# Two-stage normalising tiles, a last FFN-out block by interleaved token halves, and a ring of their own for the queries, in a one-core transformer layer

## The chip, the cores and the metric

The kernel runs on one core of a Trainium2 chip. The metric is the device time of one execution in microseconds (us). A profiled execution gives the trace; several others give the times.

## The reference, cut to what matters

One layer with D = 1024, 512 latent tokens and 256 context tokens, batch 1, in float32. What the change touches is queries and keys, the gates of the recurrence, the second norm with its SwiGLU feed-forward network (FFN) of width 2816, and the final norm:

```python
qk = silu(short_conv(concat([q, k]), conv_w, conv_b))     # 4 heads of 256
S  = einsum('bhtd,bhsd->bhts', q, k) * exp(Dm - m)        # scores of a chunk
x  = x + g1 * (mix @ w_out)
h  = rmsnorm(x, norm_ffn) * (1 + sc2) + sh2
g, u = split(h @ w_ffn_in, 2)
x  = x + g2 * ((silu(g) * u) @ w_ffn_out)                 # width 2816 = 22 tiles of 128
out = rmsnorm(x, norm_final)
```

## The kernel before, in words

**Products.** Activations lie transposed: 128 features on the partitions, 512 tokens in the row. Every factor is split into a high part, rounded by ScalarE's copy to the matmul's format, and a low part, the rest, subtracted on VectorE. A product is then three matmuls, high by high, high by low, low by high (`mm3`, L181 to L183). Matmuls move 512 columns (all tokens) or 256 (one half of them, `HALF[0]` or `HALF[1]`).

**Weights.** `wload` (line 145) has SyncE load a tile into the ring `wr` of three, ScalarE round it (L151, L164, L170) and VectorE subtract (L152, L165, L171). Its target is the ring `wh`/`wl` of two, the ring `gh`/`gl` of two ("wide"), or half tiles of `oh`/`ol`, five of each. Tiles of all these rings start at multiples of 256 bytes. Some are read from 48 elements (192 bytes) further on: the value weights (`vload`, `skip`) and the big tile `hp` of the normalised FFN input. A ring's slot is given again when all readers of its tile are done.

**Order.** Most instructions are put in order by a planner, engine by engine, from the program order and its own idea of when each is ready. Inside `manual_schedule` (the first stage, lines 242 to 364, and the first part of the FFN, lines 1091 to 1152) TensorE, ScalarE and VectorE run in the order in which the program is written; DMAs remain the planner's. On the chip each engine takes its instructions in that fixed order.

**Attention.** For each of four heads: `values`, `keys`, `attention` (two score stages, `scores`, L699 to L701, 36 matmuls of 256 columns each, key tile loaded, query tile moved), then the pooled branch, and `queries` and `keys` of the next head. Queries and keys share the ring `kq` of eleven 512-column tiles; a head takes four for its queries and six for its keys. `late_mod` streams the rows of `w_ada`, 512 KB at a time, into `pb` and multiplies them on VectorE (L496). `gates` works on small tiles [128 x 48], each with a place of its own, and writes `g_rows` to DRAM, from where `decays` reads it back.

**FFN-in.** `norm_tile(k, c, r, full)` makes one 128 x 256 tile of the normalised input: VectorE multiplies (L910), ScalarE adds the shift and rounds (L912, the high part), VectorE subtracts (L913, the low part), ScalarE writes the unrounded tile (L914). It runs eight times for the first half of the tokens under the planner, and eight times for the second half inside the manual stretch (lines 1102 to 1105). The first three of 22 feed-forward tiles run there, each by halves (`Half`: gate, up, silu, mul, low). Then come the others, by one level of Strassen's scheme (`prepare`, `front`, `back`, `strassen`), seven products of 256 columns in place of eight. It needs sums of quarters of the input (`total`: N1, N2, T3, T4), each one VectorE pass and then one split on ScalarE and VectorE. The unrounded quarters "11" and "21" lie in the ring `ur` of two, in which `prepare` also loads one of its two weight tiles.

**FFN-out** follows in three blocks, after tiles 8, 15 and 22. `ffn_out(j, c, w, c0, c1)` multiplies one output tile, adds it into `x1` (L1166) and, in the last block, adds its square to the final norm's sum (`st2`, L206, L210). Six output tiles of the last block are run over all 512 columns, tiles 6 and 7 by halves. `final(i, sd)` normalises one half of the tokens (eight VectorE instructions, L1198) and stores it. The first half's `final` comes in the middle of the last product:

```python
    for j in (6, 7):
        ffn_out(j, HALF[0], wl_[j], c0, c1)
    ffn_out(6, HALF[1], wl_[6], c0, c1)
    sd = st2.rstd_cols(HALF[0])
    ffn_out(7, HALF[1], wl_[7], c0, c1, lambda: final(0, sd))
    final(1, st2.rstd_cols(HALF[1]))
```

Of the kernel before, what the change touches and what calls it, by code (L numbers as in the profile page):

```python
# [9 lines left out]
F32 = mybir.dt.float32  # L10
F32R = mybir.dt.float32r
# [19 lines left out]
BUFS = {"a": 24, "tmp": 7, "kq": 11, "E": 6, "Sp": 10, "m": 7, "pm": 4, "act": 16, "x1": 8, "oh": 5, "ol": 5}  # L31
# [17 lines left out]
def layer_kernel(ctx: ExitStack, tc, xT, cT, w0, w1, wv0, wv, wada_a, wada_b, par, crow, bg, wpool,  # L49
# [34 lines left out]
    open_pool("kqp", ("kq",))  # L84
# [57 lines left out]
    def wide(tag, bufs=2):  # L142
        return tl(tag, [P, D], F32R, bufs, LINE)

    def wload(src, n, dst=None, skip=0):

        raw = tl("wr", [P, WMAX], F32, 3)
        nc.sync.dma_start(raw[:, :n], src)
        if dst is None:
            wh, wl = (tl(t, [P, WMAX], F32R, 2, LINE)[:, skip:skip + n] for t in ("wh", "wl"))  # L150
            nc.scalar.copy(wh, raw[:, :n])  # L151
            V.tensor_sub(wl, raw[:, :n], wh.bitcast(F32))  # L152
            return [(wh[:, i * P:(i + 1) * P], wl[:, i * P:(i + 1) * P]) for i in range(n // P)], wh, wl
        if dst == "wide":
            h, l = wide("gh"), wide("gl")
            split(raw[:, :n], h[:, :n], l[:, :n])
            return [(h[:, i * P:(i + 1) * P], l[:, i * P:(i + 1) * P]) for i in range(n // P)], None, None
        if isinstance(dst, str):
            dst = (dst, dst)
        parts = []  # L160
        for c in range(0, n, T):
            m = min(T, n - c)
            h, l = (S(t, F32R) for t in dst)
            nc.scalar.copy(h[:, :m], raw[:, c:c + m])  # L164
            V.tensor_sub(l[:, :m], raw[:, c:c + m], h[:, :m].bitcast(F32))  # L165
            parts += [(h[:, i * P:(i + 1) * P], l[:, i * P:(i + 1) * P]) for i in range(m // P)]
        return parts, None, None
# [226 lines left out]
    def queries(h):  # L394
        return [conv_part(lat_tile(Q0 + 2 * h + dk), T, 2 * h + dk) for dk in range(2)]
# [158 lines left out]
    def gates():  # L554
# [7 lines left out]
        ab, u, w, w2, pl, lf = (E(n, (P, NGC)) for n in ("g_ab", "g_u", "g_w", "g_w2", "g_pl", "g_lf"))  # L562
# [44 lines left out]
        MLb = E("g_MLb")  # L607
# [14 lines left out]
        rows = E("g_rows", (32, P))  # L622
# [3 lines left out]
        gx, c1, em = E("g_gx"), E("g_c1"), E("g_em")  # L626
# [5 lines left out]
        G = E("g_G")  # L632
# [274 lines left out]
    def norm_tile(k, c, r, full):  # L907

        t = S("tmp")[:, :TC]
        V.scalar_tensor_tensor(t, x1[k][:, c], sc2[:, k:k + 1], r, ALU.mult, ALU.mult)  # L910
        h, l = hpart(c)[k]
        nc.scalar.activation(h, t, AF.Identity, bias=sh2[:, k:k + 1])  # L912
        V.scalar_tensor_tensor(l, t, sh2[:, k:k + 1], h.bitcast(F32), ALU.add, ALU.subtract)  # L913
        nc.scalar.activation(full, t, AF.Identity, bias=sh2[:, k:k + 1])  # L914
# [134 lines left out]
    whole = {"11": [tl("ur", [P, D], F32, 2)]}  # L1049
    whole["21"] = [tl("ur", [P, D], F32, 2)]  # L1050
    for nm in ("11", "21"):
        whole[nm] = [whole[nm][0][:, :T], whole[nm][0][:, T:]]
    r = st1.rstd_rows(sd, HALF[0])
    for k in range(KT):
        norm_tile(k, HALF[0], r, whole_at(("11", "21")[k // 4], k % 4))
# [35 lines left out]
    with tc.manual_schedule(engines={mybir.EngineType.PE, mybir.EngineType.Activation, mybir.EngineType.DVE}):  # L1091
# [10 lines left out]
        norm_tile(0, HALF[1], r, whole_at("12", 0))  # L1102
        e.low()
        for k in range(1, KT):
            norm_tile(k, HALF[1], r, whole_at(("12", "22")[k // 4], k % 4))
            if k == 4:
                f.silu()
# [8 lines left out]
        e.silu()  # L1116
        t3 = total(("12", T3), lambda i: V.tensor_sub(w12[i], w22[i], w12[i]))
        n2 = total(("22", N2), lambda i: V.scalar_tensor_tensor(w22[i], w11[i], -1.0, w22[i], ALU.mult, ALU.subtract))
        wg2 = wload(wffi[4], D)[0]
        e.mul()  # L1120
# [7 lines left out]
        t4 = total(("21", T4), lambda i: V.scalar_tensor_tensor(w21[i], w22[i], -1.0, w21[i], ALU.mult, ALU.subtract))  # L1128
# [7 lines left out]
        t3()  # L1136
# [3 lines left out]
        t4()  # L1140
# [16 lines left out]
    def ffn_out(j, c, w, c0, c1, after_first=None):  # L1157

        turn_[0] += 1
        acc = banks[turn_[0] % 3]  # L1160
        m = 4 if after_first else c1 - c0
        mm3(acc[:, c], w[:m], half(act[c0:c0 + m], c), last=m == c1 - c0)
        if after_first:
            after_first()
            mm3(acc[:, c], w[m:], half(act[c0 + m:c1], c), first=False)
# [5 lines left out]
    def wchunk(j, c0, c1, dst=None):  # L1171
        return wload(wffo[j][:, c0 * P:c1 * P], (c1 - c0) * P, dst)[0]
# [123 lines left out]
```

## Time and profile before

| | |
|---|---|
| median of 3 runs | 912.81 us (907.91 to 913.37) |
| profiled execution | 911.29 us, span of its instructions 909.5 us |
| TensorE (PE) busy | 881.7 us, 97% of the span |
| VectorE (DVE) busy | 613.0 us, 67% |
| ScalarE (ACT) busy | 428.1 us, 47% |
| DMA | 121.18 MB, 133 GB/s on average |
| mean granted TensorE clock | 0.992 of full |

Times in rows count from the span's first instruction. PE is TensorE's matmuls, PEld its weight loads, DVE VectorE, ACT ScalarE, POOL GpSimd, SP SyncE, which issues most DMAs. A bracket at a row's end is the engine's idle time just before it and what ended that. The shown end of a matmul is modelled and overlaps the next one; the spacing of starts is what counts.

### The profile page before, as it was taken

What the parts mean: (1) busy time and instruction counts of PE and PEld (TensorE: products, weight loads), DVE (VectorE), ACT (ScalarE), POOL (GpSimd) and SP (SyncE); (2) the same over time, 40 slices, a digit from 0 to 9 for tenths busy, and PEclk for the clock granted to TensorE, in tenths of its full rate; (3) what the DMA queues carried; (4) which work ended last, traced back from release to release, by engine and by line L of the source; (5) the groups of instructions that cost most, each with busy time, mean ns of one, the idle gap of its engine ahead of it and who ended that gap; (6) DMA issues with size and microseconds to landing.
All of it is one profiled execution on the core that took longest, in us unless ns stands there. A gap on an engine that the chain in (4) does not pass through costs nothing.

```text
span 909.5 us, 14723 instructions
## 1 busy us (share of the span) xinstructions
PE 881.7 (97%) x5757; PEld 793.9 (87%) x5757; DVE 613.0 (67%) x1188; ACT 428.1 (47%) x806; POOL 63.3 (7%) x92
## 2 busy tenths in 40 slices
PE   8999989999999999999999899999999999999995
PEld 7689888899888998889987798989789998899985
DVE  3678665856688666886778676785366754866454
ACT  4464353545343553335543356574145741666330
POOL 0000010010001000000000000020011100111000
PEclk9999999999999999999999999999999999999998
DMA  8843031322166312762048730485355643766222
GB/s 333 324 139 115 27 79 58 116 59 81 50 214 217 99 39 78 230 226 87 27 152 280 251 117 24 134 206 126 93 153 145 153 118 88 201 140 141 55 61 93
DMA packets 42485, 121.18 MB, mean 133 GB/s; under 512 B 4625, under 2 KB 9393, under 8 KB 41393
## 3 DMA queue, kind: packets, MB, share of 16 engines
q1 hardware_dynamic: 36944, 110.29, 37.4%
q0 software_dynamic: 5472, 9.96, 6.7%
q8 instruction: 45, 0.74, 0.3%
q14 instruction: 24, 0.19, 0.1%
HBM read 116.55 MB, written 3.69 MB: 132 GB/s over the span
## 4 chain that ended last, share of the span: by engine, by line
PE 73%; DVE 11%; DMA 9%; issue 3%; ACT 3%; POOL 0%; SPq 0%; POOLq 0%; DVEq 0%; ACTq 0%
PE ps L181 15%; PE ps L183 15%; PE ps L182 15%; DMA pb<-in_wada_b 7%; PE pat L326 3%; PE ps L538 2%; PE ps L539 2%; PE ps L537 2%; DVE wl L152 2%; PE pat L741 2%; PE pat L181 2%; PE pat L182 2%; PE pat L183 2%; PE pat L739 2%; PE pat L740 2%
## 5 line engine op out<-in xcount | busy, mean ns | idle before, releaser
L151 ACT CAST wh<-wr 128x1024 fp32r<-128x1024 f32 (+3 forms) x82 | 82.7, 1009 | 134.8 <-PE ps L182 94.8
L181 PE MATMUL ps<-a,wh 128*128 128x512 f32 (+1 forms) x368 | 138.8, 377 | 0.0
L182 PE MATMUL ps<-a,wh 128*128 128x512 f32 (+1 forms) x368 | 138.5, 376 | 0.0
L183 PE MATMUL ps<-a,wl 128*128 128x512 f32 (+1 forms) x368 | 138.4, 376 | 0.0
L152 DVE TENSOR_TENSOR wl<-wr,wh 128x1024 fp32r<-128x1024 f32 (+3 forms) x82 | 96.4, 1177 | 39.9 <-ACT wh L151 38.2
L183 PE MATMUL ps<-act,wl 128*128 128x512 f32 (+1 forms) x210 | 80.7, 384 | 3.3 <-DVE wl L152 3.3
L181 PE MATMUL ps<-act,wh 128*128 128x512 f32 (+1 forms) x210 | 80.5, 383 | 0.7 <-ACT wh L151 0.7
L182 PE MATMUL ps<-act,wh 128*128 128x512 f32 (+1 forms) x210 | 80.4, 383 | 0.0
L183 PEld LDWEIGHTS ps<-a,wl 128*128 128x128 f32 x368 | 69.3, 188 | 12.7
L181 PEld LDWEIGHTS ps<-a,wh 128*128 128x128 f32 x368 | 69.3, 188 | 12.0
L182 PEld LDWEIGHTS ps<-a,wh 128*128 128x128 f32 x368 | 69.3, 188 | 11.9
L538 PE MATMUL ps<-wl,a 128*128 128x256 f32 (+1 forms) x192 | 54.3, 283 | 2.6 <-DVE wl L152 2.5
L537 PE MATMUL ps<-wh,a 128*128 128x256 f32 (+1 forms) x192 | 54.1, 282 | 0.9 <-DVE tmp L374 0.9
L539 PE MATMUL ps<-wh,a 128*128 128x256 f32 (+1 forms) x192 | 54.0, 281 | 0.0
L957 POOL DMA_DIRECT2D ol<-in_wffi x38 | 33.5, 889 | 260.6 <-ACT ol L956 118.9
L181 PE MATMUL ps<-hp,gh 128*128 128x256 f32 x176 | 50.2, 285 | 0.9 <-ACT tmp L999 0.9
L183 PEld LDWEIGHTS ps<-act,wl 128*128 128x128 f32 x210 | 39.9, 190 | 11.9 <-DVE wl L152 4.6
L1166 DVE SCALAR_TENSOR_TENSOR x<-ps,lb,x 128x512 f32<-128x512 f32 (+1 forms) x26 | 18.4, 709 | 46.3 <-PE ps L183 46.3
L183 PE MATMUL ps<-hp,gl 128*128 128x256 f32 x176 | 49.1, 279 | 0.5 <-DVE gl L171 0.5
L182 PE MATMUL ps<-hp,gh 128*128 128x256 f32 x176 | 49.0, 279 | 0.0
L496 DVE SCALAR_TENSOR_TENSOR pb<-pb,crow_s 128x1024 f32<-128x1024 f32 x32 | 39.1, 1223 | 14.6 <-DMA pb<-in_wada_b 14.2
L181 PEld LDWEIGHTS ps<-act,wh 128*128 128x128 f32 x210 | 39.9, 190 | 8.5 <-ACT wh L151 1.2
(296 smaller groups left out, 2484.4 us busy)
## 6 DMA issues: line engine op xcount, KB each, us to landing
wr<-in_w SPq DMA_DIRECT2D x42, 512.0 KB, 3.5
pb<-in_wada_b SPq DMA_DIRECT2D x32, 512.0 KB, 4.5
wr<-in_wffi SPq DMA_DIRECT2D x25, 512.0 KB, 4.0
ur<-in_wffi SPq DMA_DIRECT2D x19, 512.0 KB, 4.0
ol<-in_wffi POOLq DMA_DIRECT2D x38, 256.0 KB, 5.1
ada<-in_wada_a SPq DMA_DIRECT2D x8, 1024.0 KB, 8.3
wr<-in_wffo SPq DMA_DIRECT2D x16, 448.0 KB, 3.4
x<-in_xT SPq DMA_DIRECT2D x16, 256.0 KB, 5.7
```

The source lines that it names most:

```text
L151: nc.scalar.copy(wh, raw[:, :n])
L152: V.tensor_sub(wl, raw[:, :n], wh.bitcast(F32))
L181: nc.tensor.matmul(dst, wh, ah, start=first and i == 0, stop=False, skip_group_check=on)
L182: nc.tensor.matmul(dst, wh, al, start=False, stop=False, skip_group_check=on)
L183: nc.tensor.matmul(dst, wl, ah, start=False, stop=last and i == n - 1, skip_group_check=on)
L326: nc.tensor.matmul(acc0[i], w_first[k][i][w], aT[k][x], start=k + w + x == 0, stop=k == KT - 1 and w == 1)
L496: V.scalar_tensor_tensor(wa[:, :D], wa[:, :D], 0.5, crow_s, ALU.mult, ALU.mult, accum_out=mods[:, i:i + 1])
L537: nc.tensor.matmul(acc[:, :n], ah, wh, start=kk == 0, stop=False)
L538: nc.tensor.matmul(acc[:, :n], ah, wl, start=False, stop=False)
L539: nc.tensor.matmul(acc[:, :n], al, wh, start=False, stop=kk == KT - 1)
L957: nc.gpsimd.dma_start(l, dram, accum_op=ALU.add)
L1166: V.scalar_tensor_tensor(x1[j][:, c], acc[:, c], g2[:, j:j + 1], x1[j][:, c], ALU.mult, ALU.add)
```

## The change

It has four parts.

1. The norm is cut into `norm_first` (L910's multiply) and `norm_rest`; in VectorE's order the multiply of tile k+1 now stands ahead of the low part of tile k, and ScalarE writes the unrounded tile ahead of that low part.
2. The unrounded quarters "11" and "21" move from `ur` to the tile `sg`. T4's sum is written to two tiles of `tmp`, ahead of `e.mul`, and the splits of T3 and T4 come ahead of the second `f.mul`, no longer inside the first `prepare`. `e.silu` comes after two of the sums.
3. Queries get a ring `q` of four tiles, read from 48 elements on; `kq` shrinks from eleven to seven. To make room, `gates` uses five of its small tiles a second time, and `g_rows` becomes a tile of `tmp`.
4. In the last FFN-out block all eight weight tiles are loaded into places in which they stay for both halves; all products run by halves of 256 columns, interleaved, and the first half's `final` stands ahead of two whole products. Six of the eight weight tiles start 16 elements (64 bytes) into their places; tiles 4 and 5, in `oh`/`ol`, don't.

```diff
-BUFS = {... "kq": 11, ...}
+BUFS = {... "kq": 7, "q": 4, ...}
@@ wload
-            h, l = wide("gh"), wide("gl")
-            split(raw[:, :n], h[:, :n], l[:, :n])
+            h, l = (wide(t)[:, skip:skip + n] for t in ("gh", "gl"))
+            split(raw[:, :n], h, l)
@@ queries
-        return [conv_part(lat_tile(Q0 + 2 * h + dk), T, 2 * h + dk) for dk in range(2)]
+        return [conv_part(lat_tile(Q0 + 2 * h + dk), T, 2 * h + dk,
+                          [tl("q", [P, T + NEXT], F32R, BUFS["q"], LINE)[:, NEXT:] for _ in range(2)]) for dk in range(2)]
@@ gates
+        free = [E(n) for n in ("g_ab", "g_u", "g_w", "g_w2", "g_pl")]
+        ab, u, w, w2, pl = (flat(t) for t in free)
-        MLb = E("g_MLb")
+        MLb = free[0]
-        rows = E("g_rows", (32, P))
+        rows = S("tmp")[:32, :P]
-        gx, c1, em = E("g_gx"), E("g_c1"), E("g_em")
+        gx, c1, em = free[1:4]
-        G = E("g_G")
+        G = free[4]
@@ FFN-in
+    def norm_first(k, c, r):
         t = S("tmp")[:, :TC]
         V.scalar_tensor_tensor(t, x1[k][:, c], sc2[:, k:k + 1], r, ALU.mult, ALU.mult)
+        return t
+    def norm_rest(k, c, t, full, between):
         h, l = hpart(c)[k]
         nc.scalar.activation(h, t, AF.Identity, bias=sh2[:, k:k + 1])
+        nc.scalar.activation(full, t, AF.Identity, bias=sh2[:, k:k + 1])
+        t2 = between()
         V.scalar_tensor_tensor(l, t, sh2[:, k:k + 1], h.bitcast(F32), ALU.add, ALU.subtract)
-        nc.scalar.activation(full, t, AF.Identity, bias=sh2[:, k:k + 1])
+        return t2
+    def norm_tiles(c, r, at, also=lambda k: None):
+        t = norm_first(0, c, r)
+        for k in range(KT):
+            t = norm_rest(k, c, t, at(k), lambda: norm_first(k + 1, c, r) if k < KT - 1 else None)
+            also(k)
...
-    whole = {"11": [tl("ur", [P, D], F32, 2)]}
-    whole["21"] = [tl("ur", [P, D], F32, 2)]
+    sg0 = tl("sg", [P, 2 * D], F32, 1, LINE)
+    whole = {nm: [sg0[:, (2 * q + i) * T:(2 * q + i + 1) * T] for i in range(2)] for q, nm in enumerate(("11", "21"))}
...
         n1()
-        e.silu()
         t3 = total(("12", T3), ...)
         n2 = total(("22", N2), ...)
+        e.silu()
         wg2 = wload(wffi[4], D)[0]
+        whole["t4"] = [S("tmp") for _ in range(2)]
+        t4 = total(("t4", T4), lambda i: V.scalar_tensor_tensor(whole["t4"][i], w22[i], -1.0, w21[i], ALU.mult, ALU.subtract))
         e.mul()
...
         pw.append((wg2, wload(wffi[5], D)[0], act_tiles(2)))
-        t4 = total(("21", T4), ...)
+        t3()
+        t4()
         f.mul()
...
         p = prepare(NP)
         next(p)
-        t3()
         next(p)
         e.silu()
         next(p)
-        t4()
         e.mul()
@@ last FFN-out block
-    for j in range(6):
-        ffn_out(j, ALL, wchunk(j, c0, c1), c0, c1)
-    wl_ = {j: wchunk(j, c0, c1, ("oh", "ol")) for j in (6, 7)}
+    wl_ = [wchunk(j, c0, c1, (None, None, "wide", "wide", ("oh", "ol"), ("oh", "ol"), None, None)[j], 16) for j in range(KT)]
+    for j in range(4):
+        ffn_out(j, HALF[0], wl_[j], c0, c1)
+    for j in range(4):
+        ffn_out(j, HALF[1], wl_[j], c0, c1)
+        ffn_out(j + 4, HALF[0], wl_[j + 4], c0, c1)
+    ffn_out(4, HALF[1], wl_[4], c0, c1)
+    sd = st2.rstd_cols(HALF[0])
+    ffn_out(5, HALF[1], wl_[5], c0, c1)
+    final(0, sd)
     for j in (6, 7):
-        ffn_out(j, HALF[0], wl_[j], c0, c1)
-    ffn_out(6, HALF[1], wl_[6], c0, c1)
-    sd = st2.rstd_cols(HALF[0])
-    ffn_out(7, HALF[1], wl_[7], c0, c1, lambda: final(0, sd))
+        ffn_out(j, HALF[1], wl_[j], c0, c1)
     final(1, st2.rstd_cols(HALF[1]))
```

## Rows read from the trace of the kernel before

**Rows 1.** The page, part 1: busy us, share of the span, instructions.

```profile
PE 881.7 (97%) x5757; PEld 793.9 (87%) x5757; DVE 613.0 (67%) x1188; ACT 428.1 (47%) x806; POOL 63.3 (7%) x92
```

**Rows 2.** Windows: start:end, length, busy (instructions) by engine, PE clock, DMA, GB/s.

```profile
500.00:600.00 100.00, 93.76 (x686) 87.58 (x687) 73.67 (x135) 55.63 (x107) 5.95 (x7) 0.98 0.46 142
```

**Rows 3.** Timeline (start, us, engine, line, names, shapes), VectorE, the second half's norm.

```profile
552.06 0.48 DVE L910 SCALAR_TENSOR_TENSOR tmp<-x,sc,pat 128x256 f32<-128x256 f32 x1
553.12 0.48 DVE L913 SCALAR_TENSOR_TENSOR act<-tmp,lb,act 128x256 fp32r<-128x256 f32 x1 [0.58 <-ACT act L912]
...
563.63 0.48 DVE L913 SCALAR_TENSOR_TENSOR hp<-tmp,lb,hp 128x256 fp32r<-128x256 f32 x1 [0.58 <-ACT hp L912]
```

**Rows 4.** Timeline, ScalarE, the first half's norm: tiles 1 and 7.

```profile
541.02 0.51 ACT L912 ACTIVATE hp<-tmp,lb 128x256 fp32r<-128x256 f32 x1
...
545.84 0.49 ACT L912 ACTIVATE hp<-tmp,lb 128x256 fp32r<-128x256 f32 x1
```

**Rows 5.** Timeline, TensorE, beside the second half's norm.

```profile
558.95 0.40 PE L1176 MATMUL pat<-hp 128*128 128x512 f32 x1
...
567.02 0.29 PE L181 MATMUL ps<-hp,wh 128*128 128x256 f32 x1
```

**Rows 6.** Windows: two microseconds inside that stretch.

```profile
563.00:565.00 2.00, 2.00 (x8) 1.40 (x8) 1.42 (x5) 1.31 (x3) 0.00 (x0) 0.55 0.00 0
```

**Rows 7.** Timeline, TensorE, the second Strassen tile's first products.

```profile
591.64 0.39 PE L183 MATMUL ps<-hp,ol 128*128 128x256 f32 x1 [0.77 <-DVE ol L954]
...
593.93 0.38 PE L181 MATMUL ps<-hp,gh 128*128 128x256 f32 x1 [0.87 <-ACT tmp L999]
...
594.92 0.38 PE L183 MATMUL ps<-hp,gl 128*128 128x256 f32 x1 [0.49 <-DVE gl L171]
```

**Rows 8.** Windows: from the end of that norm to those products.

```profile
564.00:595.00 31.00, 28.86 (x234) 28.11 (x233) 25.73 (x43) 19.30 (x37) 3.68 (x4) 0.96 0.48 126
```

**Rows 9.** Timeline, TensorE: one score stage, first matmul, and the matmul after it.

```profile
206.37 0.28 PE L699 MATMUL pat<-kq,kq 128*128 128x256 f32 x1
...
210.68 0.40 PE L181 MATMUL ps<-a,wh 128*128 128x512 f32 x1
```

**Rows 10.** Timeline, TensorE: value products of two heads, and what follows the second.

```profile
189.41 0.28 PE L537 MATMUL ps<-wh,a 128*128 128x256 f32 x1
...
300.07 0.28 PE L537 MATMUL ps<-wh,a 128*128 128x256 f32 x1
...
311.30 0.28 PE L699 MATMUL pat<-kq,kq 128*128 128x256 f32 x1
```

**Rows 11.** Timeline, TensorE, last FFN-out block: 512 columns, 256 columns, last of (6, second half).

```profile
856.86 0.39 PE L181 MATMUL ps<-act,wh 128*128 128x512 f32 x1
...
885.42 0.28 PE L181 MATMUL ps<-act,oh 128*128 128x256 f32 x1
...
892.85 0.28 PE L183 MATMUL ps<-act,ol 128*128 128x256 f32 x1
```

**Rows 12.** Timeline, VectorE and TensorE, the end.

```profile
893.17 0.48 DVE L1166 SCALAR_TENSOR_TENSOR x<-ps,lb,x 128x256 f32<-128x256 f32 x1 [1.06 <-PE ps L183]
...
895.49 3.22 DVE L1198 SCALAR_TENSOR_TENSOR wr<-x,parm,pat 128x256 f32<-128x256 f32 x8 [0.86 <-PE pat L232]
...
896.24 0.28 PE L183 MATMUL ps<-act,ol 128*128 128x256 f32 x1
...
898.63 0.48 DVE L1166 SCALAR_TENSOR_TENSOR x<-ps,lb,x 128x256 f32<-128x256 f32 x1
```

**Rows 13.** Waits of TensorE: who for whom, us in total, times, longest.

```profile
PE pat L739 <- ACT Sp L170: 1.0, 1, 1.0
```

**Rows 14.** Timeline, VectorE and TensorE, a pass over `pb` and what follows.

```profile
290.28 1.23 DVE L496 SCALAR_TENSOR_TENSOR pb<-pb,crow_s 128x1024 f32<-128x1024 f32 x1 [2.64 <-DMA pb<-in_wada_b]
...
293.80 0.39 PE L538 MATMUL ps<-wl,a 128*128 128x256 f32 x1 [1.63 <-DVE wl L152]
```

**Rows 15.** The page, part 6: DMA issues, KB each, median us to landing.

```profile
pb<-in_wada_b SPq DMA_DIRECT2D x32, 512.0 KB, 4.5
```

More of the change, by code (lines that the diff above doesn't have):

```diff
@@ L29 @@
 NG = 16
-BUFS = {"a": 24, "tmp": 7, "kq": 11, "E": 6, "Sp": 10, "m": 7, "pm": 4, "act": 16, "x1": 8, "oh": 5, "ol": 5}
+BUFS = {"a": 24, "tmp": 7, "kq": 7, "q": 4, "E": 6, "Sp": 10, "m": 7, "pm": 4, "act": 16, "x1": 8, "oh": 5, "ol": 5}
 LINE = 256
@@ L83, in layer_kernel @@
     open_pool("mix", ("m", "pm", "pa", "pb"), "right")
-    open_pool("kqp", ("kq",))
+    open_pool("kqp", ("kq", "q"))
     open_pool("st", ("x", "cx", "ada", "row"))
@@ L561, in gates @@
         gi, gf = flat(gif[:, 0]), flat(gif[:, 1])
-        ab, u, w, w2, pl, lf = (E(n, (P, NGC)) for n in ("g_ab", "g_u", "g_w", "g_w2", "g_pl", "g_lf"))
+        free = [E(n) for n in ("g_ab", "g_u", "g_w", "g_w2", "g_pl")]
+        ab, u, w, w2, pl = (flat(t) for t in free)
+        lf = E("g_lf", (P, NGC))
         V.scalar_tensor_tensor(ab, gf, -1.0, gf, ALU.mult, ALU.max)
@@ L905, in hpart @@
         return B12 + [kt(B22, k) for k in range(4)]
-    def norm_tile(k, c, r, full):
+    def norm_first(k, c, r):
         t = S("tmp")[:, :TC]
         V.scalar_tensor_tensor(t, x1[k][:, c], sc2[:, k:k + 1], r, ALU.mult, ALU.mult)
+        return t
+    def norm_rest(k, c, t, full, between):
         h, l = hpart(c)[k]
         nc.scalar.activation(h, t, AF.Identity, bias=sh2[:, k:k + 1])
+        nc.scalar.activation(full, t, AF.Identity, bias=sh2[:, k:k + 1])
+        t2 = between()
         V.scalar_tensor_tensor(l, t, sh2[:, k:k + 1], h.bitcast(F32), ALU.add, ALU.subtract)
-        nc.scalar.activation(full, t, AF.Identity, bias=sh2[:, k:k + 1])
+        return t2
[4 more added lines that the diff above has]
+            also(k)
     whole = {}
@@ L1048, in layer_kernel @@
     proj_out(NW + 1, wo[NW + 1], HALF[1])
-    whole = {"11": [tl("ur", [P, D], F32, 2)]}
-    whole["21"] = [tl("ur", [P, D], F32, 2)]
-    for nm in ("11", "21"):
-        whole[nm] = [whole[nm][0][:, :T], whole[nm][0][:, T:]]
+    sg0 = tl("sg", [P, 2 * D], F32, 1, LINE)
+    whole = {nm: [sg0[:, (2 * q + i) * T:(2 * q + i + 1) * T] for i in range(2)] for q, nm in enumerate(("11", "21"))}
     r = st1.rstd_rows(sd, HALF[0])
-    for k in range(KT):
-        norm_tile(k, HALF[0], r, whole_at(("11", "21")[k // 4], k % 4))
+    norm_tiles(HALF[0], r, lambda k: whole_at(("11", "21")[k // 4], k % 4))
     for j in range(NW + 2, KT):
@@ L1101, in layer_kernel @@
         f.up()
[L1102 to L1107, printed above, removed]
+        norm_tiles(HALF[1], r, lambda k: whole_at(("12", "22")[k // 4], k % 4),
+                   lambda k: {0: e.low, 4: f.silu}.get(k, int)())
         f.mul()
@@ L1127, in layer_kernel @@
         pw.append((wg2, wload(wffi[5], D)[0], act_tiles(2)))
-        t4 = total(("21", T4), lambda i: V.scalar_tensor_tensor(w21[i], w22[i], -1.0, w21[i], ALU.mult, ALU.subtract))
+        t3()
+        t4()
         f.mul()
@@ L1155, in layer_kernel, with ffn_out @@
     turn_ = [0]
-    def ffn_out(j, c, w, c0, c1, after_first=None):
+    def ffn_out(j, c, w, c0, c1):
         turn_[0] += 1
         acc = banks[turn_[0] % 3]
[L1161 to L1165, printed above, removed]
+        mm3(acc[:, c], w, half(act[c0:c1], c))
         V.scalar_tensor_tensor(x1[j][:, c], acc[:, c], g2[:, j:j + 1], x1[j][:, c], ALU.mult, ALU.add)
@@ L1169, in ffn_out, with wchunk @@
                 st2.add(x1[j][:, c_], c_)
-    def wchunk(j, c0, c1, dst=None):
-        return wload(wffo[j][:, c0 * P:c1 * P], (c1 - c0) * P, dst)[0]
+    def wchunk(j, c0, c1, dst=None, skip=0):
+        return wload(wffo[j][:, c0 * P:c1 * P], (c1 - c0) * P, dst, skip)[0]
     for i in range(4, 8):
```

## The prediction

> **What bounds the kernel.** I began with the busy shares: TensorE is busy 97% of the span, VectorE 67% [rows 1]. Little can be won by feeding TensorE; what can be won is in the stretches where it stalls, in the pace of its matmuls, and at the end, where it has nothing left to do. So I looked through the windows for stretches in which its busy time falls short, and found one: 500 to 600 us, 93.8 of 100 us busy, clock 0.98 [rows 2]. Then the timeline of each engine inside it, then the spacing of matmul starts by tile, then the tail.
>
> In that stretch the second half's norm sets the pace. The reader is to see in VectorE's rows that each low part (L913) comes after 0.58 us of idling for ScalarE's high part, and that the next tile's multiply stands behind it. Eight tiles take from 552.06 to the start of the last low part at 563.63 [rows 3], 1.45 us each. The first half's norm, which the planner had interleaved itself, does six tiles in 4.82 us, 0.80 each [rows 4]. TensorE meanwhile needs those tiles: from 558.95 to 567.02 it starts 4 matmuls of 512 and 24 of 256 columns [rows 5], and in the middle of it the clock lies at 0.55 of full [rows 6], so part of it ran at the lower level (1.2 GHz), after the waits. 25 to 30 us later it stalls again, three times, at the first products of the second Strassen tile, whose weights VectorE and ScalarE deliver late [rows 7].
>
> **Pace of matmuls.** 126 matmuls of 512 columns take 28.56 us, 226.7 ns each; the following 62 of 256 columns take 7.43 us, 119.8 ns each [rows 11]. Scores run at the same pace, 36 in 4.31 us, 119.7 ns [rows 9]. These have both operands at multiples of 256 bytes. The value products, whose moved tile starts 192 bytes on, take 117.8 ns in one head (144 between 189.41 and 206.37, where the scores of rows 9 start) and 113.4 in another (99 from 300.07 to 311.30) [rows 9, 10]. So an offset helps, by 1.9 or by 6.3 ns a matmul, and the operands alone don't decide which.
>
> **The change, part by part.**
>
> *Two-stage norm.* The work is the same; the order lets the multiply of tile k+1 run while ScalarE makes tile k's high part. I take the 0.80 us of the planner's order [rows 4], which holds the same four instructions. Then the last low part comes 8 x 0.65 = 5.2 us sooner. TensorE's 28 matmuls at 226.7 and 117.8 ns take 3.73 us where they took 8.07 [rows 5, 10, 11]: 4.3 us, the clock's share included, and the norm is then ahead of the gate products. Bounds: 3.5 (if the clock falls all the same, at another small wait) and 4.3; I take 4.3.
>
> *Quarters in `sg`, T3 and T4 early.* The stalls of rows 7 sum to 2.1 us of idling. `ur` is free, so the second Strassen tile's weights needn't wait for T4's split. But VectorE was busy 25.73 of the 31 us from the norm to there [rows 8], and nothing of that work goes: starting 4.4 us sooner, it keeps pace with a TensorE that is 4.3 us sooner only because some of its 5.3 us of idling goes too, and the order takes T4's split out of the stretch in which those weights are made. Bounds 0 and 2.1; I take 2.0, since the load that waited is freed outright. A wait moves: the second `f.mul` now stands behind four more splits on VectorE, and behind it the gate product of the third tile's second half, which needs its PSUM banks. Adding the durations along VectorE's queue I find it some 1.5 us ahead of TensorE there (an estimate from the rows of the queue); if that is wrong, it costs what it is late. `sg` is needed by `prepare` only after T4's sum: nothing. No DMA is added; SyncE's loads into `ur` move up, into a stretch where its queue is short.
>
> *Queries offset by 192 bytes.* 8 score stages of 36, 288 matmuls: from 119.7 to 117.8 or 113.4 is 0.5 to 1.8 us. I take 0.9: they come behind value products, which showed either pace. `q` has four tiles and no spare one, where the eleventh of `kq` was spare; the next head's queries are made a whole pooled branch after the scores, so I cost that wait at nothing.
>
> *Gates.* Reused tiles have their last readers on VectorE's own queue: nothing. `g_rows` in `tmp` may wait for a place. It leads to the first scores, where TensorE already waits 1.0 us for one tile [rows 13], and no work lies beside it. Bounds 0 and 1.0; I take 0, as it is the nearer (a ring of seven, three of them taken by the gates and their constants).
>
> *Last block, TensorE.* Before: 126 x 226.7 + 84 x 119.8 ns = 38.6 us. After: 336 matmuls of 256 columns; 252 of them read weights 64 bytes into a 256-byte line, which is the same distance between the operands as in the value products seen from the other side; 84 don't. At 113.4 that is 28.6 + 10.1 = 38.6 us, at 117.8 it is 39.8, and if the offset does nothing 40.3 [rows 10, 11]. So 0 to 1.6 us more. I take 0.9, for the Strassen products before it, like the value products, run at either pace. The loads are the same eight; tiles 6 and 7 take the places of 0 and 1, free four products (10 us) before they are needed. More and shorter evictions lie beside matmuls.
>
> *Last block, the tail.* Now the first half's `final` holds VectorE from 895.49 for 3.22 us, and the last eviction, L1166, starts at 898.63, 2.39 us after the last matmul's start at 896.24. One product earlier it came 0.32 us after (893.17 after 892.85) [rows 11, 12]. With two whole products (2 x 2.5 us) behind `final`, 3.2 us of it fit: 2.0 us gained. Bounds 1.5 and 2.1. What follows, square, sum, root, eight multiplies, store, stays.
>
> A rule speaks about the split. The Trainium skill, "TensorE: Matmul & The Clock Gate", section "Back-to-back issue gap", gives an isolated gap of columns / 2.4 + 2.5 ns, with no regard to addresses. By that two 256-column matmuls cost 2.6 ns more than one of 512 (rows 11: 12.9 ns), the 126 splits 0.3 us instead of 1.6, and the offset nothing anywhere. The trace does not agree: it shows 119.8, 117.8 and 113.4 ns for the same columns where the formula has 109.2.
>
> **Sum**: 4.3 + 2.0 + 0.9 - 0.9 + 2.0 = 8.3 us less. The profiled execution took 911.29 us, 1.8 more than its span; so 903.0. The median stands 1.5 us above it, so 904.5, and I say 904.
>
> **Rivals.**
>
> *Fast pace throughout.* With stalls gone, more of the offset matmuls keep 113.4 ns: scores 1.8, last block 0, and so 10.1 us less; if the Strassen tiles follow, 4.4 ns each, a stretch of 500 gives 2.2 more. 900 to 902. For it: heads at the fast pace exist; against: nothing in the change sets the pace.
>
> *VectorE takes it back.* The stalls of rows 7 stay because VectorE is the bound there: 6.3 us less, 906.5. For: rows 8. Against: `ur` free.
>
> *The offset buys nothing* (the change doesn't do what it says): scores 0, last block +1.6: 4.3 + 2.0 + 2.0 - 1.6 = 6.7 less, 906. For: the slow pace of 117.8 is close to 119.7; against: the fast one. The rule of the Trainium skill's page "TensorE: Matmul & The Clock Gate" above leads here too, but for its cheap split, with which it would be 8.0 less, 905.
>
> *A worse order in attention, slower.* Outside the manual stretches the planner makes a new order, since rings and sizes changed. VectorE's passes over `pb` wait there for DMA: 2.64 us at 290.28, and 3.5 us on TensorE stalls for the weight subtraction queued behind that [rows 14]. A load lands 4.5 us after its issue [rows 15]. Where a pass is put ahead of a subtraction that TensorE needs next, up to those 4.5 us are lost. From two such places on (9.0 us) the kernel is slower than before; with three, once in each stretch that streams `pb`, it is -8.3 + 13.5 = 5.2 us more, 918; four put it past 1%. For: it happens once already; against: 32 loads, and only one such wait over 1.6 us on TensorE there.
>
> **Chances.** Less than 1% can hardly be told from no change here, so the limits are 903.7 and 921.9. The forecast 0.50, its own range 901 to 908, 0.21 of it below 903.7; fast pace 0.14, all faster; VectorE 0.13 and offset 0.12, 0.06 of them together faster; worse order 0.11, 0.04 within 1% and 0.07 slower. Faster 0.41, within 1% 0.52, slower 0.07. The range runs from the fast pace with part of Strassen's, 898, to the upper end of the two weaker gains with `g_rows` waiting and a norm gain of 3.5, and a first misplaced pass: 911. It leaves out most of the worse order and the edge of the fast pace.
>
> **What the changed profile would show.** Right: in the second half's norm, high parts 0.8 us apart with no VectorE idling of 0.58; TensorE without gaps from the first gate product to the second Strassen tile, no lowered clock there; L1166 about 0.3 us after the last matmul's start; scores under 119 ns. Wrong, and where: the gaps of rows 7 still there (VectorE); a gap at the third tile's second gate product (the moved splits); last block over 40 us (offset); new TensorE waits for L152 or L171 between 100 and 500 us (order). The forecast falls as a whole if TensorE's busy time after the norm shows new stalls as long as those removed.

## The result

In 20 runs each, the median went from 908.46 us (905.88 to 915.46) to 905.35 us (901.64 to 908.57). The ratio is 0.995, 95% interval 0.9931 to 0.9969: a gain of some 4.5 us (2.8 to 6.3), half a per cent. The profiled executions are 911.29 and 905.2 us, 6.1 us apart, where the forecast took 8.3 from the first of them. The forecast time, 904 us, is near the median; the forecast gain is not near the measured one.

The page of the changed kernel, part 1 (busy us, share of the span, instructions), answers to [rows 1]:

```profile
span 903.4 us, 14978 instructions
PE 879.0 (97%) x5883; PEld 796.5 (88%) x5883; DVE 613.9 (68%) x1194; ACT 428.3 (47%) x806; POOL 63.3 (7%) x92
```

TensorE has 126 matmuls more and is as full as before. The table cuts both spans at starts of TensorE's matmuls, so its rows add up to the spans. "Norm" runs from the first gate product of the second FFN tile to the first Strassen product (551.78 to 585.04 before), "first block" from there to FFN-out, "last block" from the first to the last FFN-out matmul of that block, "tail" to the end.

| us | before | after | difference |
|---|---|---|---|
| start to norm | 551.78 | 552.69 | +0.91 |
| norm | 33.26 | 29.29 | -3.97 |
| first Strassen block | 51.81 | 50.63 | -1.18 |
| second | 68.81 | 68.00 | -0.81 |
| third | 68.81 | 67.64 | -1.17 |
| last FFN-out block | 39.38 | 41.90 | +2.52 |
| tail | 13.25 | 10.82 | -2.43 |
| FFN-out blocks 1, 2 | 82.37 | 82.43 | +0.06 |

The timeline of VectorE in the second half's norm (start, duration, engine, line, operation, idle before it), beside [rows 3]:

```profile
557.92 0.48 DVE L912 SCALAR_TENSOR_TENSOR tmp<-x,sc,pat 128x256 f32<-128x256 f32 x1
558.49 0.48 DVE L921 SCALAR_TENSOR_TENSOR hp<-tmp,lb,hp 128x256 fp32r<-128x256 f32 x1
558.89 0.48 DVE L912 SCALAR_TENSOR_TENSOR tmp<-x,sc,pat 128x256 f32<-128x256 f32 x1
559.29 0.49 DVE L921 SCALAR_TENSOR_TENSOR hp<-tmp,lb,hp 128x256 fp32r<-128x256 f32 x1
560.09 0.49 DVE L921 SCALAR_TENSOR_TENSOR hp<-tmp,lb,hp 128x256 fp32r<-128x256 f32 x1 [0.31 <-ACT hp L918]
```

Low parts come 0.80 us apart, the multiplies fill the gaps, and the 0.58 us of idling before each is gone. TensorE's waits in this stretch are gone with it (1.06 us in the norm before, none now). The granted clock is 1.00 over the 12 us of the first row below; in the kernel before it was 0.86 from 556 to 568 us, and 0.55 in [rows 6]. Windows of the changed kernel, columns as in [rows 2]:

```profile
552.00:564.00 12.00, 12.00 (x105) 12.00 (x104) 10.81 (x25) 10.15 (x23) 0.00 (x0) 1.00 0.05 19
564.00:595.00 31.00, 29.22 (x241) 28.25 (x241) 27.18 (x44) 19.86 (x37) 4.56 (x5) 1.00 0.49 135
```

Nearly as much idling as in [rows 7], though, is still there, on the timeline of TensorE:

```profile
583.39 0.28 PE L181 MATMUL ps<-hp,gh 128*128 128x256 f32 x1
...
585.07 0.39 PE L181 MATMUL ps<-hp,oh 128*128 128x256 f32 x1
...
586.31 0.39 PE L183 MATMUL ps<-hp,ol 128*128 128x256 f32 x1 [0.73 <-DVE ol L968]
...
588.68 0.39 PE L181 MATMUL ps<-hp,gh 128*128 128x256 f32 x1 [0.94 <-ACT pat L1009]
```

Before the second row TensorE idles 0.11 us, too little for a bracket. Together it is 1.78 us, against 2.13 before, but these are not the waits of [rows 7]. Rows of ScalarE, VectorE and TensorE in the kernel before:

```profile
586.60 0.36 ACT L995 COPY pat<-ps 128x256 f32<-128x256 f32 x1 [0.53 <-PE ps L183]
590.29 0.69 DVE L969 TENSOR_TENSOR sg<-ur 128x512 f32<-128x512 f32 x1 [0.78 <-DMA ur<-in_wffi]
590.48 0.28 PE L181 MATMUL ps<-hp,oh 128*128 128x256 f32 x1
```

There the copy of the first product (L995) ran on time, VectorE did wait for the load into `ur`, just ahead of the subtraction for `ol`, and the second tile's first product (590.48) came 5.4 us after the first Strassen product, behind four products of the first tile. Now VectorE doesn't wait for that load, but the planner has also ordered TensorE anew: the second tile's first product (585.07) comes 3.1 us after the first Strassen product, behind two. Its weights are not ready, and the first tile's third product, behind it, waits for a 0.36 us copy, L1009. The timeline of ScalarE shows where that copy stood:

```profile
584.41 1.12 ACT L966 CAST oh<-wr 128x512 fp32r<-128x512 f32 x2
585.45 0.40 ACT L1097 CAST act<-tmp 128x256 fp32r<-128x256 f32 x1
585.75 0.63 ACT L970 ACTIVATE ol<-wr 128x512 fp32r<-128x512 f32 x1
586.28 0.60 ACT L966 CAST oh<-ur 128x512 fp32r<-128x512 f32 x1
586.79 0.63 ACT L970 ACTIVATE ol<-ur 128x512 fp32r<-128x512 f32 x1
587.33 1.03 ACT L170 CAST gh<-sg 128x1024 fp32r<-128x1024 f32 x1
588.26 0.36 ACT L1009 COPY pat<-ps 128x256 f32<-128x256 f32 x1
```

The product that it copies was issued in full by 583.39, where the next one starts. The copy ran at 588.26, behind the rounding of the next tile's weights. The Trainium skill, "PSUM — Partial Sum Buffer", section "Engine vs sequencer instructions", says that the queues of ScalarE, VectorE and GpSimd are strictly first in, first out; these rows agree, with 4.9 us between the two.

The last block, TensorE and VectorE, beside [rows 11]:

```profile
850.68 0.28 PE L181 MATMUL ps<-act,wh 128*128 128x256 f32 x1
...
853.48 0.50 PE L181 MATMUL ps<-act,wh 128*128 128x256 f32 x2 [0.52 <-ACT act L170]
...
854.43 0.39 PE L182 MATMUL ps<-act,wh 128*128 128x256 f32 x1 [0.33 <-DVE act L171]
```

```profile
852.69 1.08 DVE L152 TENSOR_TENSOR wl<-wr,wh 128x896 fp32r<-128x896 f32 x1
853.69 0.68 DVE L171 TENSOR_TENSOR act<-tmp,act 128x512 fp32r<-128x512 f32 x1
```

A new wait: the first output tile reaches the last FFN tile of `act` after 18 matmuls, by halves 2 us after it begins, and that tile is not yet split. On VectorE the 1.08 us subtraction for the second output tile's weights is ahead of it. By matmul starts the two waits cost 1.17 us, restarts included.

The tail, beside [rows 12]:

```profile
892.58 0.28 PE L183 MATMUL ps<-act,wl 128*128 128x256 f32 x1
892.90 0.48 DVE L1170 SCALAR_TENSOR_TENSOR x<-ps,lb,x 128x256 f32<-128x256 f32 x1
```

The last eviction starts 0.32 us after the last matmul, where it was 2.39. What follows it takes 10.50 us, where it took 10.86; that difference is not shown to be the change's, for the whole tail lies between 10.69 and 11.19 us in the kernels below that have part 4, and between 13.26 and 13.87 in those that don't.

### The profile page after: what moved, and what is told of

Its sections match the earlier page's. It is cut to its first block, busy times and chain, and to the rows that moved or that the text cites. A ratio compares the mean times of both kernels' runs of the same rounds, so it can differ in the third digit from the quotient of the medians.

```text
span 903.4 us, 14978 instructions
## 1 busy us (share of the span) xinstructions
PE 879.0 (97%) x5883; PEld 796.5 (88%) x5883; DVE 613.9 (68%) x1194; ACT 428.3 (47%) x806; POOL 63.3 (7%) x92
## 4 chain that ended last, share of the span: by engine, by line
PE 70%; DVE 13%; DMA 9%; issue 4%; ACT 4%; POOL 0%; SPq 0%; POOLq 0%; DVEq 0%; ACTq 0%
PE ps L181 14%; PE ps L183 14%; PE ps L182 14%; DMA pb<-in_wada_b 6%; DVE wl L152 3%; PE pat L326 3%; PE ps L539 2%; PE ps L540 2%; PE ps L538 2%; PE pat L744 2%; PE pat L742 2%; PE pat L743 2%; PE pat L182 2%; PE pat L181 2%; PE pat L183 2%
## 5 line engine op out<-in xcount | busy, mean ns | idle before, releaser
L151 ACT CAST wh<-wr 128x1024 fp32r<-128x1024 f32 (+3 forms) x80 | 80.8, 1012 | 120.2 <-PE ps L182 94.3
L152 DVE TENSOR_TENSOR wl<-wr,wh 128x1024 fp32r<-128x1024 f32 (+3 forms) x80 | 94.3, 1180 | 36.6 <-ACT wh L151 35.4
L183 PEld LDWEIGHTS ps<-act,wl 128*128 128x128 f32 x224 | 42.5, 190 | 10.3 <-DVE wl L152 4.3
L181 PEld LDWEIGHTS ps<-act,wh 128*128 128x128 f32 x224 | 42.4, 190 | 8.0 <-ACT wh L151 1.5
L182 PEld LDWEIGHTS ps<-act,wh 128*128 128x128 f32 x224 | 42.6, 190 | 6.7 <-DVE act L171 0.5
```

The lines of the kernel that those rows point to most:

```text
L181: nc.tensor.matmul(dst, wh, ah, start=first and i == 0, stop=False, skip_group_check=on)
L182: nc.tensor.matmul(dst, wh, al, start=False, stop=False, skip_group_check=on)
L183: nc.tensor.matmul(dst, wl, ah, start=False, stop=last and i == n - 1, skip_group_check=on)
```

## Experiments

Each kernel was run beside the kernel before on the same chip, for a ratio. These intervals are about 2 us to either side, so what separates causes below is read in the traces, stage by stage.

### Parts 1 and 2 of the change alone

The kernel before with part 1's hunks (`norm_first`, `norm_rest`, `norm_tiles`):

```diff
-        norm_tile(k, HALF[0], r, whole_at(...))
+    norm_tiles(HALF[0], r, lambda k: whole_at(...))
```

> The kernel before with part 1 alone, the two-stage norm; the unrounded quarters stay in `ur`, the splits of T3 and T4 in the first `prepare`. Both theories expect the norm's gain: high parts 0.80 us apart, no TensorE gap and no lowered clock between the first tiles of the gate product and the up product, so about 4.3 us less than before (ratio 0.995). They part at the second Strassen tile. Theory 'queues': VectorE and ScalarE, each in its fixed order, make the weights late there, so TensorE idles 1.8 to 2.5 us over its first products, as before. Rival 'load into ur': the load that waits for T4's split makes them late; with TensorE 4.3 us sooner and the load no sooner, the idling grows to 4 us or more and the net gain is 2 us.

And with part 2's as well:

```diff
-    whole = {"11": [tl("ur", [P, D], F32, 2)]}
+    sg0 = tl("sg", [P, 2 * D], F32, 1, LINE)
...
+        t3()
+        t4()
         f.mul()
```

> The kernel before with parts 1 and 2: two-stage norm, quarters in `sg`, T3 and T4 split early. Theory 'queues': freeing `ur` lets the load come sooner, but the stalls at the second Strassen tile stay at 1.6 to 2.0 us, so the time is within 0.5 us of that with part 1 alone (4 to 5 us less than before). Rival 'load into ur': stalls there under 0.5 us, and 1.5 to 2 us less than with part 1 alone (about 6 us less than before).

Measured: part 1 alone 0.9995 (0.9976 to 1.0015), no gain; parts 1 and 2 0.9948 (0.9925 to 0.9972). The norm took 28.70 us in the first and 29.20 in the second. But the first Strassen block took 54.94 and 51.42 us. The stalls on TensorE's timeline, part 1 alone, then parts 1 and 2:

```profile
583.66 0.38 PE L181 MATMUL ps<-hp,oh 128*128 128x256 f32 x1 [1.38 <-ACT oh L963]
585.67 0.38 PE L183 MATMUL ps<-hp,ol 128*128 128x256 f32 x1 [1.51 <-DVE ol L965]
587.96 0.58 PE L181 MATMUL ps<-hp,gh 128*128 128x256 f32 x1 [0.84 <-ACT pat L1006]
```

```profile
584.64 0.39 PE L181 MATMUL ps<-hp,oh 128*128 128x256 f32 x1 [0.19 <-ACT oh L963]
585.87 0.39 PE L183 MATMUL ps<-hp,ol 128*128 128x256 f32 x1 [0.73 <-DVE ol L965]
588.24 0.39 PE L181 MATMUL ps<-hp,gh 128*128 128x256 f32 x1 [0.95 <-ACT pat L1006]
```

3.73 us and 1.87 us; TensorE's order is that of the changed kernel in both. In part 1 alone, SyncE's wait ahead of the load into `ur` (L956; who for whom, us in total, times, longest), VectorE's split of T4 out of `ur`, and the load:

```profile
SPq L956 <- DVE tmp L1095: 10.0, 1, 10.0
578.09 1.29 DVE L171 TENSOR_TENSOR hp<-ur,hp 128x512 fp32r<-128x512 f32 x2 [0.60 <-ACT hp L170]
579.41 0.33 SPq L956 DMA_DIRECT2D ur<-in_wffi  x1
```

The load was issued as soon as the split ended, at 579.38 (the view names VectorE's next instruction), and the load into `wr` behind it on SyncE's queue at 580.94. So each theory was right about the cause in one kernel. With TensorE 4 us sooner, the load does make the weights late (3.73 us); with the load out of the way, the two queues still do (1.87 us). Part 1 alone pays for its stalls twice, for behind them TensorE's clock fell. Its window there, columns as in [rows 2]:

```profile
588.00:590.00 2.00, 2.00 (x9) 2.00 (x10) 1.98 (x2) 1.94 (x4) 0.00 (x0) 0.50 1.01 159
```

From 586 to 588 us it was 0.89 and from 590 to 592 0.76, with parts 1 and 2 it was 1.00 throughout. That is some 1.7 us (an estimate, 2 x 0.11 + 2 x 0.50 + 2 x 0.24); with the 1.9 us of idling it makes up the 3.5 us by which the first blocks differ. Part 2 is worth both, not because the stalls of the kernel before go, but because part 1 would have made them longer. Part 2 without part 1 was not run.

### Part 3 alone

```diff
-BUFS = {... "kq": 11, ...}
+BUFS = {... "kq": 7, "q": 4, ...}
```

> The kernel before with part 3 alone: queries in a ring of their own, 192 bytes into their places, gates' tiles reused. Theory 'pace by place': scores at 113 to 115 ns each instead of 119.7, 288 of them, so 1.4 to 1.9 us less than before; stalls in the attention as before within 1 us. Rival 'planner's order': the gain in the changed kernel's scores hangs on nothing, but new waits of VectorE or ScalarE on TensorE in 100 to 500 us take back 1 us or more, so no change or slower.

Measured: 0.9989 (0.9968 to 1.001). The 288 scores took 32.99 us by their starts, against 34.49 before and 33.00 with the whole change: 1.5 us less, in stages of 113.3 to 113.6 ns a matmul, two of eight at 117.8. TensorE's waits between the first and the last score stage sum to 4.6 us, against 5.9 before and 3.9 with part 4 alone, whose instructions there are those of before: no new wait. 'Pace by place' holds in the trace; the ratio is too coarse for 1.5 us.

### Part 4 alone

```diff
-    for j in range(6):
-        ffn_out(j, ALL, wchunk(j, c0, c1), c0, c1)
+    for j in range(4):
+        ffn_out(j, HALF[0], wl_[j], c0, c1)
...
```

> The kernel before with part 4 alone: last block by interleaved halves, all weights kept. Theory 'halves cost more than priced': the block's matmuls take 2.5 to 3 us more (252 at 117 to 118 ns, and the first product, by halves, comes to the last FFN tile about 2 us after its start and waits for it about 1.2 us), the tail is 2.1 us shorter, so 0.4 to 1 us more than before. Rival 'as predicted': the block 0.9 us more, the tail 2.0 less, so 1.1 us less than before, with no wait of TensorE for the last FFN tile; the wait seen in the changed kernel then came from the stages ahead of it, not from the halves.

Measured: 1.0003 (0.9984 to 1.0022). The block took 42.22 us (+2.84), the tail 11.19 (-2.06), so 0.8 us more, and TensorE waits for `act` with nothing changed ahead of it; by matmul starts these waits cost 1.8 us:

```profile
861.00 0.50 PE L181 MATMUL ps<-act,wh 128*128 128x256 f32 x2 [1.18 <-ACT act L170]
861.96 0.38 PE L182 MATMUL ps<-act,wh 128*128 128x256 f32 x1 [0.33 <-DVE act L171]
```

'Halves cost more than priced' holds: the last block bought its shorter tail at more than its price.

### Four wide tiles in the last block

The changed kernel with

```diff
     for j in range(4):
-        ffn_out(j, HALF[0], wl_[j], c0, c1)
-    for j in range(4):
-        ffn_out(j, HALF[1], wl_[j], c0, c1)
-        ffn_out(j + 4, HALF[0], wl_[j + 4], c0, c1)
+        ffn_out(j, ALL, wl_[j], c0, c1)
+    for j in range(4, 8):
+        ffn_out(j, HALF[0], wl_[j], c0, c1)
```

> The changed kernel, but the last block's first four output tiles run over all 512 columns; tiles 4 to 7 by halves as in the change, with the first half's `final` still ahead of two whole products. Theory 'halves': the first product then comes to the last FFN tile some 4 us after its start instead of 2, so the 1.2 us lost there go, and 84 pairs of 256-column matmuls become one of 512 (about 9 ns each, 0.8 us); the tail stays at 10.5 us. Block 40.0 to 40.6 us instead of 42.2, and some 2 us less than the changed kernel: ratio to before about 0.993. Rival 'as predicted': the wait came from the stages ahead and stays; only 0.8 us come back.

Measured: 0.9958 (0.9927 to 0.9989). The wait for `act` is gone and the block takes 40.32 us by the table's cut, 1.58 less than in the changed kernel, the tail 10.69. So 'halves' holds in the trace for the wait. Its other price was wrong: the 84 matmuls of 512 columns took 233.3 ns each, 2 ns less than two of 256 at 117.8, where 9 were expected. In [rows 11], with both operands at multiples of 256 bytes, they took 226.7: here the offset of 64 bytes costs them 6.6 ns each. The ratio shows no gain over the change, and can't exclude 1.6 us.

### Back to multiples of 256 bytes

```diff
-... tl("q", [P, T + NEXT], F32R, BUFS["q"], LINE)[:, NEXT:] ...
+... tl("q", [P, T + NEXT], F32R, BUFS["q"], LINE)[:, :T] ...
-    wl_ = [wchunk(j, c0, c1, (...)[j], 16) for j in range(KT)]
+    wl_ = [wchunk(j, c0, c1, (...)[j], 0) for j in range(KT)]
```

> The changed kernel with queries and the last block's weights back at multiples of 256 bytes (rings, order and sizes unchanged). Theory 'the place in memory sets the pace': scores 119 to 120 ns again (1.6 us more than the changed kernel), the last block's matmuls 119.5 instead of 117.5 (0.5 us more): 2 us more, ratio to before about 0.997. Rival 'the pace is set by what runs before, not by the place': scores stay near 113 to 114 ns, no change.

Measured: 0.9991 (0.9967 to 1.0015). Scores 34.51 us in stages of 119.5 to 120.0 ns, none faster; the last block 42.78 us, 0.88 more, of which 0.36 is a longer wait for `act`. The place sets the scores' pace: 1.5 us. By the Trainium skill's formula for the isolated gap in "TensorE: Matmul & The Clock Gate", section "Back-to-back issue gap", which has no place in it, nothing should have changed; the traces disagree, with 119.8 ns here and 113.5 in the changed kernel for the same instructions.

### The copy ahead of the weights

The changed kernel with, in `strassen`,

```diff
             f = front(j, p) if j < hi else None
+            if f:
+                next(f)
             if j + 1 < hi:
                 p = prepared(j + 1)
...
             if f:
-                next(f)
                 next(f)
```

> The changed kernel, but in `strassen` the first step of `front` (the copy of the first product out of PSUM, L1009) is written ahead of the next tile's weight preparation. Theory 'queue order': TensorE's wait of 0.94 us for that copy at the second Strassen tile goes, and so one part of the 1.8 us of stalls; the waits for `oh` and `ol` (0.8 us) stay or grow by the copy's 0.5 us: 0.3 to 0.9 us less than the changed kernel. Rival 'VectorE's load': the total of the stalls there stays at 1.8 us, only its place moves.

Measured: 0.992 (0.9897 to 0.9942). The three stalls are gone, and there is another of 0.74 us, for the next copy, L1013. ScalarE, then TensorE:

```profile
583.75 0.36 ACT L1009 COPY pat<-ps 128x256 f32<-128x256 f32 x1
...
587.91 1.04 ACT L170 CAST wh<-sg 128x1024 fp32r<-128x1024 f32 x1
588.85 0.36 ACT L1013 COPY tmp<-ps 128x256 f32<-128x256 f32 x1
...
589.27 0.39 PE L181 MATMUL ps<-hp,gh 128*128 128x256 f32 x1 [0.74 <-ACT tmp L1013]
```

The copy ran 1.0 us after its product was issued in full, where it was 4.9; the next one still stands behind roundings. The waits for `oh` and `ol` went too, which the theory expected to stay: with this edit TensorE's order is again that of the kernel before, the second tile's first product behind four. The first block took 48.93 us, 1.70 less than in the changed kernel; 1.04 of it is idling, the rest pace. The idling is 0.74 us in the two further kernels with this edit as well, and 1.8 to 1.9 in the three without it. So 'VectorE's load' falls: the load is the same, and the sum fell. 'Queue order' holds in the sense that an order, not a load, made the stalls; how much of the 1.04 is ScalarE's order and how much TensorE's isn't shown apart.

> The changed kernel with both of these edits (four wide tiles in the last block, copy first). If the two are independent, the sum of their gains: 2.3 to 2.9 us less than the changed kernel, ratio to before about 0.992. If the stalls only move ('VectorE's load') and the wait for the last FFN tile stays, 0.8 us less.

Both edits together: 0.9919 (0.989 to 0.9948). First block 48.95 us, last block 40.33, as in the two kernels with one edit each. They don't add up in full, though: with the copy alone the last block was already down to 41.06 us (the first of its two waits nearly gone, a part of it at the fast pace), so the wide tiles add 0.7 there, and the ratio is no better than with the copy alone. And the third Strassen block took 69.25 us, as with the copy alone (69.26), against 67.64: 1.6 us given back. The starts show why. After FFN-out its 588 matmuls begin at 117 to 118 ns, and with the copy first there is no break in them. In the changed kernel a weight load waits 0.18 us for the copy after 24 matmuls, and behind that they run at 113.3. The block's first matmul, the weight load that waits, the matmul behind it, and the first matmul after the block, changed kernel:

```profile
783.04 0.28 PE L181 MATMUL ps<-hp,oh 128*128 128x256 f32 x1
...
786.01 0.19 PEld L181 LDWEIGHTS ps<-hp,gh 128*128 128x128 f32 x1 [0.18 <-ACT pat L1009]
786.01 0.39 PE L181 MATMUL ps<-hp,gh 128*128 128x256 f32 x1
...
850.68 0.28 PE L181 MATMUL ps<-act,wh 128*128 128x256 f32 x1
```

So one more kernel, with both edits, but the old order in the first tile of the third block:

```diff
+            late = j == lo == 15
-            if f:
+            if f and not late:
                 next(f)
...
             if f:
+                if late:
+                    next(f)
                 next(f)
```

> The kernel with both edits (copy first, four wide tiles), but in the third Strassen block the first tile keeps the old order, the copy behind the next tile's weight preparation. In that kernel the third block's 588 matmuls ran without a break, all at 118 ns, 69.25 us; in the changed kernel they had a break of 0.18 us after 23 matmuls (a weight load waiting for that copy) and ran at 113.3 ns behind it, 67.64 us. Theory 'a break sets the pace, which then holds until the next': the break comes back after 23 matmuls, some 560 matmuls behind it run at 113.3 ns, the block takes 67.0 to 67.4 us, 2 us less than with both edits. Rival 'the pace of a stretch has nothing to do with the break': the block stays at 69 us or falls by other amounts, and the pace changes at places without a break.

Measured: 0.9851 (0.9822 to 0.9881), median 900.26 us, the lowest of all. The break came back, in the same place and of the same length, and behind it the pace stayed slow:

```profile
778.86 0.28 PE L181 MATMUL ps<-hp,oh 128*128 128x256 f32 x1
...
781.83 0.19 PEld L181 LDWEIGHTS ps<-hp,gh 128*128 128x128 f32 x1 [0.18 <-ACT pat L1009]
781.84 0.38 PE L181 MATMUL ps<-hp,gh 128*128 128x256 f32 x1
...
848.37 0.40 PE L181 MATMUL ps<-act,wh 128*128 128x512 f32 x1
```

69.50 us for the block, and 69.75 for the second: the expectation of 67 was wrong. What survives of the theory: through all the traces a long stretch of Strassen products keeps one pace, 113.3 or 117 to 118 ns, and changes it only at a break (up to 588 matmuls without one). What falls is that a given break gives a given pace. Its first block, with the same 0.74 us of idling, took 50.45 us at the slow pace, where 48.95 was measured with both edits. Nor does the trace explain this kernel's ratio: from the norm on it is 3.6 us longer than with both edits (0.9919), and it was already 6 us ahead at the norm (546.99 against 552.95 us), where every engine has the same instructions in the same order. TensorE idled 9.0 us up to there, against 12.5, and the clock from 510 to 515 us was 1.00, against 0.66. What makes the one execution wait less than the other is left open.

### The copy ahead of the weights, before the change

The same hunk in the kernel before.

> The kernel before with nothing but the copy-first order in `strassen`. Theory 'queue order': the part of the stalls at the second Strassen tile that waits for ScalarE's copies (about 0.9 of 2.1 us) goes, and with it most breaks between the products, so 0.5 to 1 us less before the first FFN-out block. Rival 'the load into `ur` is the only cause there before the change': stalls stay at 2.1 us, since the copies stand behind a load that comes late.

Measured: 0.9984 (0.9962 to 1.0007). Two of three stalls stay:

```profile
596.93 0.39 PE L181 MATMUL ps<-hp,gh 128*128 128x256 f32 x1 [0.86 <-ACT tmp L999]
597.91 0.39 PE L183 MATMUL ps<-hp,gl 128*128 128x256 f32 x1 [0.49 <-DVE gl L171]
```

1.35 of 2.13 us; the first, for `ol`, went. The first block took 49.82 us, 1.99 less, of which 0.78 is idling and the rest pace. Neither theory fits, and the edit isn't shown to have taken even that stall: with part 3 alone and part 4 alone, whose orders in this block are those of the kernel before, the wait for `ol` was 0 and 0.50 us, the other two as ever. It goes with how late VectorE gets the load into `ur` (0.78 us of waiting in the kernel before, 0.51 with part 4 alone, none with part 3 alone). The copy that the edit moves had run on time already, at 586.60 in the kernel before, so there was little to take. Block two from its 36th matmul on and all of block three ran without a break at the slow pace, 69.74 and 69.25 us, which took 1.4 us back.

## Why the prediction was right, and where it was not

That the time came out near 904 is luck. The forecast started from 912.81 us, the median of three runs; the median of 20 is 908.46. The gain worked out was 8.3 us; the measured one is 4.5, and its interval, up to 6.3, leaves 8.3 out. In the two traces the five terms of the sum come to 5.7 us (4.0 + 0.35 + 1.5 - 2.5 + 2.4). What was not in the sum, 2.8 us of pace gained in the Strassen blocks and 2.4 us lost ahead of the norm, nearly cancels. Two of the signs that were to show the forecast wrong are there: the idling of [rows 7], and a last block of 41.90 us, over 40.

- **Two-stage norm, 4.3 us**: the norm took 3.97 us less, and 4.56 and 4.06 in the two kernels without parts 3 and 4 (part of their spread is pace). Right, mechanism and size: high parts 0.8 us apart, no gap, no lowered clock.
- **Quarters in `sg`, 2.0 us**: this step failed. It took the stalls of [rows 7] to go, "since the load that waited is freed outright". The idling went from 2.13 to 1.78 us. The load stood behind the first stall of [rows 7] (0.77 us, and none in a kernel in which it landed in time), not behind all three; and the new order of TensorE and ScalarE made others, of which 1.04 us went with the copy written first. Part 2's worth, 1.9 us of idling and some 1.7 of lowered clock, is real, but only against a kernel with part 1 alone, which I had not priced: there the stalls grow to 3.73 us. "VectorE takes it back" had the outcome nearly right, with the wrong reason: it was an order, not a load.
- **Queries, 0.9 us**: mis-sized, 1.5 us, inside its bounds. Six of eight stages took the fast pace, where I had placed it in the middle.
- **Last block, 0.9 us more**: mis-sized, 2.5 us, outside its bounds of 0 to 1.6. Pace makes 1.1 (252 matmuls at 117.8 and 84 at 119.8 ns against [rows 11]), the wait for `act` 1.2. I had counted when weights are needed, not when the last FFN tile is: by halves, the first product gets there in 2 us instead of 4.
- **Tail, 2.0 us**: 2.07 for the eviction, as worked out. The 0.36 behind it lies within what the tail differs by from kernel to kernel.
- **Gates, 0**: no new wait in the attention (4.4 us between the first and the last score stage, 5.9 before), and part 3 alone wasn't slower; the rival with a worse order did not happen.
- **Not in the sum**: 2.0 us less in the second and third Strassen blocks, whose code did not change. In the changed kernel nearly all their products ran at 113.3 ns; this is the first rival's "if the Strassen tiles follow", but the runs do not show that the change brings it: parts 3 and 4 alone, with the Strassen code of before, took 67.6 us for the third block too, and the kernel above with the change and the best ratio 69.50. The first block's 1.18 us is 0.35 of idling and 0.8 of pace. Against it, 0.9 us more before the norm, in spite of 1.5 us gained in the scores. Two low clocks can account for that: a mean of 0.94 instead of 0.97 in the first 60 us, and, behind a wait of 2.1 us of TensorE for weights that both kernels have (to 510.42 and 509.62 us), 0.66 instead of 1.00. They are worth up to 1.8 and 1.7 us, an estimate (60 x 0.03 and 5 x 0.34). Part of the second window ran at the lower level, 1.2 GHz, in one and not in the other; a shorter wait ahead of that of 2.1 us was 0.73 us before and 1.04 after. The window of before, then that of after:

```profile
510.00:515.00 5.00, 4.58 (x20) 3.82 (x21) 2.27 (x4) 1.78 (x3) 0.00 (x0) 1.00 0.84 265
```

```profile
510.00:515.00 5.00, 5.00 (x17) 3.93 (x16) 2.36 (x4) 1.89 (x4) 0.00 (x0) 0.66 0.87 277
```

Across the kernels of this study the norm's start lies between 546.99 and 555.16 us. Six of them, the changed one and the five made from it, have the same instructions in the same order on every engine up to there (one reads the queries from another place), and still lie 6.0 us apart. That is more than any one part gave, and why stages were compared.

In the working itself: the formula quoted there gives 2.5 ns for a split, not 2.6. The 4.4 us by which VectorE was to start sooner come from no row; the sum above them has 5.2. The lower end of the range, 898, is 2 us below what the rival that it is taken from gives.

## What to carry to other kernels

When an engine is made to arrive sooner, price the stall behind it twice: what it was, and what it becomes if its cause stays where it is. On an engine that serves a critical consumer, look whether the short instruction that frees it stands behind the long preparation of the next tile. Written ahead, it took 1.0 us of idling here, at no cost in buffers, with TensorE's order changed by the same edit; in the kernel before, where that copy was on time already, it gave nothing that shows. And when a planner orders the engines, compare their orders before and after, not only their waits. When a product is cut into halves, ask for each operand how much sooner its last piece is needed.

## What the runs showed of the hardware

- The same 256-column matmul came at 113.3, 117 to 118 or 119.8 ns. In the scores, with both operands at multiples of 256 bytes, only the last was seen (119.5 to 120.1 in all 48 stages of six kernels); with the moved one 192 bytes on, either of the first two (113.3 to 113.6 or 117.7 to 117.8 in all 48 stages of the six others). With weights 64 bytes on, in the last block, either of the first two as well.
- At 512 columns weights 64 bytes on made it slower: 233.3 ns, in the three kernels with four wide tiles in the last block, against 226.7 with both operands at multiples of 256 bytes.
- In the Strassen blocks, with the moved operand 192 bytes on, the pace holds until a break in the stream. It lasted for 588 matmuls at 118 ns (69.25 us a block) and for 553 at 113.3 (67.30 us). A break of 0.18 us can change it, but the same break was followed by the fast pace in the changed kernel and by the slow one in another. This alone moves a run by about 2 us a block. In the last block the pace changed without a break too: with part 4 alone it was 113.4 ns ahead of 21 matmuls with weights at a multiple of 256 bytes (120.0), and 117.8 behind them.
